# Norms behind the attention by a broadcast ones-product and a wide power on GpSimd, and FFN operands prepared 728 columns at a time

## The chip, the cores and the metric

One core of a Trainium2 chip runs one program. A core has TensorE (PE, matrix products; its weight loads are listed apart as PEld), VectorE (DVE), ScalarE (ACT), GpSimd (POOL) and SyncE (SP), which issues the DMAs here. Each engine executes its own queue in order; engines wait for one another by semaphores. The metric is the device time of the program in microseconds (us), median of three runs; the span is the time from the first to the last instruction in one profiled execution.

## What is computed

One step of a one-layer encoder over 2048 prompt frames and 8 x 16 sample frames, 2176 columns in all, model width 1024, in F32:

```
h   = RMSNorm(x);  p = h @ w_in                       # u, v | q, k, v
A   = u * (tril(W_s) LN(v) + b)                       # gating in chunks of 128
B   = stick-breaking attention, 8 heads x 64          # causal; samples have a cache
mix = concat(RMSNorm(A), RMSNorm(B)) @ w_out;  x += RMSNorm(mix)
up  = RMSNorm(x) @ w_up;  up_c = causal conv, width 3 (per column of up)
x  += RMSNorm((gelu(up_c[:, :2816]) * up_c[:, 2816:]) @ w_down)
# RMSNorm(x) = x * rsqrt(mean(x*x) + 1e-6) * gain
```

## The kernel before

Activations lie transposed: the 128 partitions hold features, the free axis holds frames (columns), so a norm is a sum over partitions and over the feature tiles. A product of full precision is three products of rounded halves (`mm3`: hi x hi, hi x lo, lo x hi), and so every weight tile is split after its load: ScalarE copies the high half (L184), VectorE subtracts it (L185, both inputs in SBUF).

The program has four phases. Phase 1 projects, phase 2 is the attention with the gating filled in between its products; phase 3, the mix stage (from about 1133 us), forms the mix and the residual x1 over six pieces of columns (five of 384, one of 256); phase 4, the FFN (first product at 1347.53 us), goes over three blocks of 726 or 728 columns. A block runs 44 ups (one weight tile each: the product into PSUM `pu`, convolution taps on VectorE L1112) and 40 downs in five groups, whose products are added into the SBUF tile `acc`, of which there is one.

Jobs (one weight tile and its products) run in a list order (`drive`); between jobs, generators in `chains` are each advanced one `yield` by `tick`. A chain's `yield`s therefore set how many jobs lie between its steps in the program; a scheduler then places each engine's instructions.

The norms are such chains. A square is taken on ScalarE and added up over the feature tiles (`sq_step`, L256, mostly on GpSimd) into a tile `acc` of 128 x n. `rstd_chain` then makes the factors in a compact form: per 128 columns one product of the sums with a 128 x 64 block of ones (L209) puts the sums of 128 columns on 128 partitions, one column wide; VectorE makes mean + eps (L212, 128 x m, m at most 4); GpSimd takes the power -0.5 of these m columns (L216); VectorE spreads each over a diagonal (L228, and L231 for the low half); one or two products with ones (L236) bring the factors to all partitions and n columns in PSUM (`rb`), from where VectorE's scalings read them. The chains behind the attention that use it:

- `mix_prep_chain`: norm of a piece of attention output `ob` (scaling L959, residue L963), beside the mix products of the piece before;
- `x1_chain`: norm of the mix (scaling L984, residual add on GpSimd L987);
- `h2_chain`: norm of x1 for the first FFN block (scaling L1010, residues L1016);
- `ffn_prep_chain`: for the next FFN block, first four norms of 182 columns each (`norm_chain`), then, once the last reader of the old operands is done, the operands: for each of four sub-blocks of 182 columns it fetches all 8 feature tiles of x1 and scales, copies and subtracts tile by tile (L920, L923, L924);
- `y_chain` and `y_last_chain`: norm of the FFN output in two parts (scalings L1218 and L1193 in place in `acc`, residual adds, then the stores).

`KEEP` names the tiles of w_out that stay in SBUF through phase 3; the others are fetched and split again for each piece.

Of the kernel before, what the change touches and what calls it, by code (L numbers as in the profile page):

```python
# [34 lines left out]
EPS = 1e-6  # L35
# [18 lines left out]
def hybrid_kernel(ctx: ExitStack, tc: tile.TileContext, a: dict):  # L54
    nc = tc.nc
    dma = nc.sync.dma_start
# [14 lines left out]
    ones = cpool.tile([P, P], F32, name="ones")  # L71
# [127 lines left out]
    def rstd_chain(pool, pspool, key, acc, n, width, shared=None, w=None):  # L199

        starts = [min(s, n - P) for s in range(0, n, P)]
        m = len(starts)
        sh = m * P - n
        yield
        out = pspool.tile([P, 512], F32, tag="st" + key, name="rb", bufs=1)
        for i, s in enumerate(starts):
            nc.tensor.matmul(out[:, 64 * i:64 * i + 64], lhsT=acc[:, s:s + P], rhs=ones[:, 0:64],  # L209
                             start=True, stop=True)  # L210
        var = pool.tile([P, 4], F32, tag="var" + key, name="var", bufs=2)
        nc.vector.tensor_scalar(  # L212
            out=var[:, :m], in0=out[:, :64 * m].rearrange("p (m t) -> p m t", t=64)[:, :, 0],
            scalar1=1.0 / width, scalar2=EPS, op0=ALU.mult, op1=ALU.add)
        r = pool.tile([P, 4], F32, tag="rstd" + key, name="rstd", bufs=2)
        nc.gpsimd.tensor_tensor(out=r[:, :m], in0=var[:, :m], in1=mhalf[:, :m], op=ALU.pow)  # L216
        yield
        yield
        if shared:
            yield from lock(shared)  # L220
        tag = shared or "dg" + key
        parts = 2 if w else 1
        dg = pool.tile([P, 2, w], F32R, tag=tag, name="dg", bufs=1) if w else pool.tile(
            [P, 1, 384], F32, tag=tag, name="dg", bufs=1)
        for i in range(m):
            o = sh if i == m - 1 else 0
            c = slice(i * P, (i + 1) * P - o)
            nc.vector.tensor_scalar(out=dg[:, 0, c], in0=ident[:, o:], scalar1=r[:, i:i + 1],  # L228
                                    scalar2=None, op0=ALU.mult)
            if w:  # L230
                nc.vector.scalar_tensor_tensor(out=dg[:, 1, c], in0=ident[:, o:], scalar=r[:, i:i + 1],  # L231
                                               in1=dg[:, 0, c].bitcast(F32), op0=ALU.mult, op1=ALU.subtract)
        yield
        yield
        for i in range(parts):
            nc.tensor.matmul(out[:, :n], lhsT=onesr if w else ones, rhs=dg[:, i, :n],  # L236
                             start=(i == 0), stop=(i == parts - 1))
        held.discard(shared)
        return r, out

    def norm_chain(pool, pspool, key, src, nk, n, width):
        acc = pool.tile([P, 182], F32, tag="sqa" + key, name="sqa", bufs=1)
        for k0 in range(0, nk, 4):
            sq_sum(pool, key, acc, src[:, k0:k0 + 4, :n], k0 == 0, n)
            yield
        yield
        return (yield from rstd_chain(pool, pspool, key, acc, n, width, w=182))[1]

    def sq_step(pool, key, acc, src, first, n, eng=None):

# [9 lines left out]
    def lock(key):  # L260
# [2 lines left out]
            yield  # L263
        held.add(key)

    def mm3(ps, whi, wlo, ahi, alo, start, stop):
        nc.tensor.matmul(ps, lhsT=whi, rhs=ahi, start=start, stop=False)  # L267
        nc.tensor.matmul(ps, lhsT=whi, rhs=alo, start=False, stop=False)  # L268
        nc.tensor.matmul(ps, lhsT=wlo, rhs=ahi, start=False, stop=stop)  # L269


    kqs = ExitStack()
# [619 lines left out]
    def ffn_prep_chain(pool, pspool, fb, out, free):  # L892

        s0, n0, n1 = FBLK[fb]
        subs = [(o, min(182, n0 + n1 - o)) for o in range(0, n0 + n1, 182)]
        rbs = pool.tile([P, 728], F32, tag="rbs", name="rbs", bufs=1)

        def fetch_x1(off, n):
            x = pool.tile([P, KD, 182], F32, tag="xp", name="xp")
            for src, o0, o1 in x1_s.parts(s0 + off, s0 + off + n):  # L900
                dma(x[:, :, o0:o1], src.rearrange("k p n -> p k n"))
            return x

        for off, n in subs:
            yield from lock("b")
            x = fetch_x1(off, n)
            yield
            rb = yield from norm_chain(pool, pspool, "b", x, KD, n, D)
            nc.vector.tensor_copy(rbs[:, off:off + n], rb[:, :n])
            held.discard("b")  # L910
        nxt = fetch_x1(*subs[0])
        while not free():
            yield
        hhi = hpool.tile([P, KD, 728], F32R, tag="hhi", name="hhi")
        hlo = hpool.tile([P, KD, 728], F32R, tag="hlo", name="hlo")
        for i, (off, n) in enumerate(subs):
            x, nxt = nxt, fetch_x1(*subs[i + 1]) if i + 1 < len(subs) else None
            for k in range(KD):
                hi, lo = hhi[:, k, off:off + n], hlo[:, k, off:off + n]
                tc.keep_in_program_order(nc.vector.scalar_tensor_tensor(  # L920
                    out=x[:, k, :n], in0=x[:, k, :n], scalar=cvec[:, C_GPF + k:C_GPF + k + 1],
                    in1=rbs[:, off:off + n], op0=ALU.mult, op1=ALU.mult))
                nc.scalar.copy(hi, x[:, k, :n])  # L923
                (nc.gpsimd if k % 2 else nc.vector).tensor_tensor(out=lo, in0=x[:, k, :n], in1=hi.bitcast(F32),  # L924
                                                                  op=ALU.subtract)
                if k % 2:
                    yield
        out += [hhi, hlo]

    ypool = ctx.enter_context(tc.tile_pool(name="y", bufs=1, reuse_waits="tile", side="right"))  # L930
# [1 line left out]
    with ExitStack() as c3:  # L932
# [5 lines left out]
        def mix_prep_chain(pi, A):  # L938
# [15 lines left out]
            for f in range(4):  # L954
                sq_step(two, "x", acc, ob[f], f == 0, n, nc.vector)
            yield
            rb = (yield from rstd_chain(two, ps3s, "a", acc, n, 512, "dg"))[1]
            for f in range(4):
                tc.keep_in_program_order(nc.vector.scalar_tensor_tensor(  # L959
                    out=ob[f], in0=ob[f], scalar=cvec[:, C_GB + f:C_GB + f + 1], in1=rb[:, :n],  # L960
# [6 lines left out]
        def x1_chain(pi, mix, acc):  # L967
# [8 lines left out]
            x = []  # L976
            for k in range(0, 6, 2):
                fetch(k)
            yield
            rb = (yield from rstd_chain(two, ps3s, "x", acc, n, D, "dg"))[1]  # L980
            if pi < 2:
                sumb = two.tile([P, 384], F32, tag="dgb", name="sumb", bufs=1)
            for k in range(KD):
# [16 lines left out]
        def h2_chain(pi, mix, acc):  # L1000
# [2 lines left out]
            n = min(PIECES[pi][1], FBLK[1][0] + 2 - c0)  # L1003
            hhi, hlo = h2
            yield
            rb = (yield from rstd_chain(two, ps3s, "b", acc, n, D))[1]
            parts = [(0, 0, NSAMP), (NSAMP, NSAMP + 2, n - NSAMP)] if pi == 0 else [(0, c0 + 2, n)]
            for k in range(KD):
                t = two.tile([P, 384], F32, tag="h", name="h")
# [60 lines left out]
    with ExitStack() as c4:  # L1070
# [11 lines left out]
        def block_jobs(fb, h2, h2n):  # L1082
# [104 lines left out]
            def y_last_chain(acc, c, pi, ssum):  # L1187
                c0, n = c.start, c.stop - c.start
                x, t0 = st["x"], s0 + 2 + c0
                rb = (yield from rstd_chain(one, psd, "yb"[pi], ssum, n, D, w=(TAIL, 256)[pi]))[1]  # L1190
                for k in range(KD):
                    o, xk = acc[:, k, c], x[:, k, c]
                    tc.keep_in_program_order(nc.vector.scalar_tensor_tensor(  # L1193
# [10 lines left out]
            def y_chain(acc, c, pi, ssum):  # L1204
                c0, n = c.start, c.stop - c.start
                yield from lock("y")
                rb = (yield from rstd_chain(one, psd, "y", ssum, n, D, w=TAIL))[1]
                if first:
                    parts = [(0, 0, NSAMP), (NSAMP + 2, NSAMP, n - NSAMP - 2)] if pi == 0 else [(0, c0 - 2, n)]
                else:  # L1210
# [129 lines left out]
```

## Time and profile before

| | |
|---|---|
| runs | 2986.50, 2989.91, 2989.08 us; median 2989.08 |
| profiled execution | 2982.77 us, span 2981.0 us, mean granted TensorE clock 0.984 |
| busy | PE 2861.2, DVE 1893.1, ACT 1345.9, POOL 336.4 us |
| mix stage, 1133 to 1373 us | PE 233.39, DVE 167.33, ACT 118.26, POOL 118.85 of 240.00 us |
| FFN, 1373 to 2953 us | PE 1567.37, DVE 820.56, ACT 514.28, POOL 82.35 of 1580.00 us |
| last 28 us | PE 11.26, DVE 20.36, ACT 2.51, POOL 12.61 us |

All times of the rows come from the one profiled execution, whose own time is 6.3 us under the median. A row of a group gives busy time and mean duration over all of its instructions; the idle time beside it is what the engine spent waiting just before them, with the releaser. Matmuls overlap in the pipeline, so a matmul's shown duration (about 330 ns for 364 columns) is longer than the distance to the next (about 167 ns).

### The profile page before, as it was taken

To read this page: it belongs to the slowest core of one execution; us is meant where nothing else is said; L and a number is where in the kernel's file an instruction comes from. 1 tells how busy PE (TensorE), PEld (TensorE's weight loads), DVE (VectorE), ACT (ScalarE), POOL (GpSimd) and SP (SyncE) were. 2 spreads that over 40 slices of the span, in tenths; PEclk is the share of its full clock that TensorE was granted. 3 is DMA by queue.
4 is the path that set the end of the run, shared out by engine and by line. 5 is a ranking of instruction groups with operands and counts; after the bars stand their busy time and mean duration, and the time that the engine had idled before them with its cause. 6 is when DMAs were issued, how large, how long until landed. Compare 5 with 4: busy or idle time off the path is not lost.

```text
span 2981.0 us, 44269 instructions
## 1 busy us (share of the span) xinstructions
PE 2861.2 (96%) x17094; PEld 2625.7 (88%) x17094; DVE 1893.1 (64%) x2840; ACT 1345.9 (45%) x2391; POOL 336.4 (11%) x487
## 2 busy tenths in 40 slices
PE   9999988889989998999999999999999999999997
PEld 8999876657666768999999999999999989999997
DVE  7666668888988885866454455763444566344445
ACT  5445457677777764554332233433222343323232
POOL 0000011010111012562000000300000030000002
PEclk9999989999999999999999999999999999999998
DMA  7767854322433226665212212532212233221223
GB/s 253 240 231 242 260 168 124 110 86 67 133 87 106 84 70 224 216 208 174 84 58 78 65 61 69 160 118 75 67 57 64 64 115 115 78 64 54 75 64 109
DMA packets 242673, 356.06 MB, mean 119 GB/s; under 512 B 26528, under 2 KB 172192, under 8 KB 241440
## 3 DMA queue, kind: packets, MB, share of 16 engines
q1 hardware_dynamic: 242464, 353.24, 37.9%
q8 instruction: 135, 2.21, 0.3%
q14 instruction: 74, 0.61, 0.1%
HBM read 285.66 MB, written 67.51 MB: 118 GB/s over the span
## 4 chain that ended last, share of the span: by engine, by line
PE 60%; DVE 4%; DMA 2%; ACT 1%; issue 1%; POOL 0%; SPq 0%; POOLq 0%; DVEq 0%; ACTq 0%
PE pu L268 12%; PE pu L267 12%; PE pu L269 12%; PE pd L267 5%; PE pd L269 5%; PE pd L268 5%; PE psm L267 2%; PE psm L268 2%; PE psm L269 2%; PE po L724 1%; PE z L690 1%; PE pt L707 1%; DMA xp<-x_s 1%; DVE S L556 1%; DMA wr<-wdown 1%
## 5 line engine op out<-in xcount | busy, mean ns | idle before, releaser
L185 DVE TENSOR_TENSOR wlo<-wr,whi 128x1024 fp32r<-128x1024 f32 (+2 forms) x325 | 353.6, 1089 | 552.0 <-ACT whi L184 550.1
L267 PE MATMUL pu<-hhi,whi 128*128 128x364 f32 (+1 forms) x2112 | 694.8, 329 | 1.8 <-ACT nhs L1124 1.8
L268 PE MATMUL pu<-hlo,whi 128*128 128x364 f32 (+1 forms) x2112 | 695.4, 329 | 0.0
L269 PE MATMUL pu<-hhi,wlo 128*128 128x364 f32 (+1 forms) x2112 | 694.9, 329 | 0.0
L184 ACT CAST whi<-wr 128x1024 fp32r<-128x1024 f32 (+2 forms) x325 | 297.0, 914 | 699.4 <-PE pu L268 276.0
L267 PEld LDWEIGHTS pu<-hhi,whi 128*128 128x128 f32 x2112 | 398.6, 189 | 2.4 <-ACT nhs L1124 2.4
L268 PEld LDWEIGHTS pu<-hlo,whi 128*128 128x128 f32 x2112 | 398.0, 188 | 0.2 <-POOL hlo L924 0.2
L269 PEld LDWEIGHTS pu<-hhi,wlo 128*128 128x128 f32 x2112 | 397.5, 188 | 0.1
L267 PE MATMUL pd<-ghi,whi 128*128 128x362 f32 (+3 forms) x1016 | 335.8, 330 | 11.9 <-DVE acc L1160 11.8
L269 PE MATMUL pd<-ghi,wlo 128*128 128x362 f32 (+3 forms) x1016 | 334.8, 330 | 0.0
L268 PE MATMUL pd<-glo,whi 128*128 128x362 f32 (+3 forms) x1016 | 334.7, 329 | 0.0
L1112 DVE SCALAR_TENSOR_TENSOR y<-pu,cvec,y 128x726 f32<-128x726 f32 (+2 forms) x352 | 270.0, 777 | 8.7 <-ACT y L1109 4.1
L556 DVE TENSOR_TENSOR_SCAN S<-S 128x896 f32<-128x896 f32 (+8 forms) x136 | 216.6, 1596 | 28.2 <-ACT S L553 27.9
L553 ACT ACTIVATE S<-z 128x512 f32<-128x512 f32 (+3 forms) x336 | 191.2, 572 | 60.4 <-DVE left L698 17.6
L707 PEld LDWEIGHTS pt<-ident,s 128*128 128x128 f32 x1088 | 128.5, 146 | 98.5 <-ACT wT L708 39.9
L707 PE MATMUL pt<-ident,s 128*128 128x128 f32 x1088 | 177.9, 291 | 35.0 <-ACT wT L708 26.1
L690 PE MATMUL z<-K,Q 128*128 128x512 f32 (+3 forms) x640 | 198.6, 409 | 10.0 <-ACT s L554 8.7
L267 PEld LDWEIGHTS pd<-ghi,whi 128*128 128x128 f32 x1016 | 192.5, 189 | 15.4 <-DVE acc L1160 7.3
L558 DVE TENSOR_TENSOR s<-s,S 128x640 f32<-128x640 f32 (+7 forms) x200 | 179.3, 902 | 37.8 <-ACT s L554 23.0
L1160 DVE TENSOR_TENSOR acc<-acc,pd 128x362 f32<-128x362 f32 (+2 forms) x192 | 101.6, 530 | 156.5 <-PE pd L269 155.9
L708 ACT COPY wT<-pt 128x512 f32<-128x512 f32 (+3 forms) x320 | 165.2, 555 | 77.6 <-PE pt L707 75.8
L268 PEld LDWEIGHTS pd<-glo,whi 128*128 128x128 f32 x1016 | 192.3, 189 | 0.3
(212 smaller groups left out, 4938.7 us busy)
## 6 DMA issues: line engine op xcount, KB each, us to landing
wr<-wup SPq DMA_DIRECT2D x132, 512.0 KB, 3.3
wk<-win_t SPq DMA_DIRECT2D x96, 256.0 KB, 2.7
wr<-win_f SPq DMA_DIRECT2D x40, 512.0 KB, 5.0
wr<-wout SPq DMA_DIRECT2D x38, 512.0 KB, 4.1
wr<-wdown SPq DMA_DIRECT2D x72, 256.0 KB, 2.7
x<-xT SPq DMA_DIRECT2D x40, 384.0 KB, 5.1
wr<-wdown SPq DMA_DIRECT2D x48, 320.0 KB, 2.9
Q<-q_s SPq DMA_DIRECT2D x112, 128.0 KB, 4.6
```

The costliest lines, as they stand in the source:

```text
L184: nc.scalar.copy(hi, wr)
L185: nc.vector.tensor_tensor(out=lo, in0=wr, in1=hi.bitcast(F32), op=ALU.subtract)
L267: nc.tensor.matmul(ps, lhsT=whi, rhs=ahi, start=start, stop=False)
L268: nc.tensor.matmul(ps, lhsT=whi, rhs=alo, start=False, stop=False)
L269: nc.tensor.matmul(ps, lhsT=wlo, rhs=ahi, start=False, stop=stop)
L553: nc.scalar.activation(S[:, c0:c0 + cn], z, AF.Sigmoid, scale=-1.0)
L556: nc.vector.tensor_tensor_scan(out=R, data0=R, data1=R, initial=1.0 if carry is None else carry, op0=ALU.mult, op1=ALU.bypass)
L558: nc.vector.tensor_tensor(out=s[:, :W], in0=s[:, :W], in1=S[:, 1:W + 1], op=ALU.mult)
L690: nc.tensor.matmul(z, lhsT=Q[:, j, i * P:(i + 1) * P], rhs=K2[:, b0 * P + c0:b0 * P + c0 + cn], start=(j == 0), stop=(j == 1 and not diago ...
L707: nc.tensor.transpose(pt[:, j], st["w"][:, (j0 - b0 + j) * P:(j0 - b0 + j + 1) * P], ident)
L708: nc.scalar.copy(shared["T", pr, j0, g][:, :jn, i * P:(i + 1) * P], pt[:, :jn])
L1112: nc.vector.scalar_tensor_tensor(out=o, in0=i, scalar=w, in1=o, op0=ALU.mult, op1=ALU.add)
```

## The change

Behind the attention the compact form is replaced by `bcast_chain`. One F32 product of a full 128 x 128 block of ones with the sums over all n columns gives the sum of every column on every partition; VectorE makes mean + eps over n columns from PSUM into an SBUF tile `rw`; GpSimd takes the power of these 128 x n in place; the scalings read `rw` from SBUF. No diagonals are made and no second product. The norms of phase 1 keep `rstd_chain`. The widths are 384 (256 in the last piece, 340 for the second part of the first FFN block's operands), 182, 362 and 364, and 470 and 256 in the last block.

The products of the 182-column norms are issued behind the newest block product (`newest`). In `ffn_prep_chain` the second part now fetches two feature tiles over all 728 columns (`fetch_pair`) and scales, copies and subtracts each over 728 columns: 8 steps of 728 columns in place of 32 of 182, the same elements. Its very first fetch goes through `load`, which keeps the order of the weight loads. `KEEP` loses one tile. Both `rw` and a 128 x 470 tile of -0.5 are new in SBUF.

```diff
+    mhalfw = cpool.tile([P, 470], F32, name="mhalfw")
+    nc.gpsimd.memset(mhalfw, -0.5)
+
+    def bcast_chain(pool, pspool, key, acc, n, width, w):
+
+        yield
+        out = pspool.tile([P, 512], F32, tag="st" + key, name="rb", bufs=1)
+        with tc.issue_after(newest[0]) if w == 182 else ExitStack():
+            nc.tensor.matmul(out[:, :n], lhsT=ones, rhs=acc[:, :n], start=True, stop=True)
+        r = pool.tile([P, w], F32, tag="rw" + key, name="rw", bufs=1)
+        nc.vector.tensor_scalar(out=r[:, :n], in0=out[:, :n], scalar1=1.0 / width, scalar2=EPS, op0=ALU.mult,
+                                op1=ALU.add)
+        nc.gpsimd.tensor_tensor(out=r[:, :n], in0=r[:, :n], in1=mhalfw[:, :n], op=ALU.pow)
+        yield
+        yield
+        return r
...
-        return (yield from rstd_chain(pool, pspool, key, acc, n, width, w=182))[1]
+        return (yield from bcast_chain(pool, pspool, key, acc, n, width, 182))
...
+        newest[:] = [nc.tensor.matmul(ps, lhsT=wlo, rhs=ahi, start=False, stop=stop).ins]
...
-            x = fetch_x1(off, n)
+            x = fetch_x1(off, n, dma if off else load)
...
+        def fetch_pair(k):
+            x = pool.tile([P, KD * 182], F32, tag="xp", name="xw").rearrange("p (k n) -> p k n", k=2)
+            for src, o0, o1 in x1_s.parts(s0, s0 + total):
+                dma(x[:, :, o0:o1], src[k:k + 2].rearrange("k p n -> p k n"))
+            return x
...
-        for i, (off, n) in enumerate(subs):
-            x, nxt = nxt, fetch_x1(*subs[i + 1]) if i + 1 < len(subs) else None
-            for k in range(KD):
-                hi, lo = hhi[:, k, off:off + n], hlo[:, k, off:off + n]
+        for k0 in range(0, KD, 2):
+            x, nxt = nxt, fetch_pair(k0 + 2) if k0 + 2 < KD else None
+            for j in range(2):
+                k, xk = k0 + j, x[:, j, :total]
+                hi, lo = hhi[:, k, :total], hlo[:, k, :total]
...
-            rb = (yield from rstd_chain(two, ps3s, "a", acc, n, 512, "dg"))[1]
+            rb = yield from bcast_chain(two, ps3s, "a", acc, n, 512, 384)
...
-            rb = (yield from rstd_chain(two, ps3s, "x", acc, n, D, "dg"))[1]
+            rb = yield from bcast_chain(two, ps3s, "x", acc, n, D, 384)
...
-            rb = (yield from rstd_chain(two, ps3s, "b", acc, n, D))[1]
+            rb = yield from bcast_chain(two, ps3s, "b", acc, n, D, 384)
...
-        KEEP = (0, 2)
+        KEEP = (0,)
...
-                rb = (yield from rstd_chain(one, psd, "yb"[pi], ssum, n, D, w=(TAIL, 256)[pi]))[1]
+                rb = yield from bcast_chain(one, psd, "yb"[pi], ssum, n, D, (TAIL, 256)[pi])
...
-                rb = (yield from rstd_chain(one, psd, "y", ssum, n, D, w=TAIL))[1]
+                rb = yield from bcast_chain(one, psd, "y", ssum, n, D, TAIL)
```

In the new kernel the line numbers are others: the wide mean + eps is L252 and the wide power L254, the square sums L274, the residual add of the mix L1014, its scaling L1011, the taps L1139, the scalings of the y chains L1245 and L1220, the last residual adds L1224. Three places of the instruction order follow.

GpSimd in the mix stage, in the kernel before, from the norm of the second piece of `ob` on (`rstd` is the narrow power's result, `sumx` the mix's sum of squares, `mix<-x,mix` the residual adds):

```order
L216 TENSOR_TENSOR rstd<-var,mhalf 128x3
L256 TENSOR_TENSOR sumx<-sumx,sq_12132 128x384
L216 TENSOR_TENSOR rstd<-var,mhalf 128x3
L256 TENSOR_TENSOR sumx<-sumx,sq_12179 128x384
L987 TENSOR_TENSOR mix<-x,mix 128x384 x8
L256 TENSOR_TENSOR sumx<-sumx,sq_12237 128x384
L256 TENSOR_TENSOR sumx<-sumx,sq_12301 128x384
L256 TENSOR_TENSOR sumx<-sumx,sq_12347 128x384
L256 TENSOR_TENSOR sumx<-sumx,sq_12384 128x384
L216 TENSOR_TENSOR rstd<-var,mhalf 128x3
```

The same stretch of GpSimd in the changed kernel (`rw` is the tile of n factors):

```order
L254 TENSOR_TENSOR rw<-rw,mhalfw 128x384
L274 TENSOR_TENSOR sumx<-sumx,sq_12121 128x384
L254 TENSOR_TENSOR rw<-rw,mhalfw 128x384
L1014 TENSOR_TENSOR mix<-x,mix 128x384 x8
L274 TENSOR_TENSOR sumx<-sumx,sq_12179 128x384
L274 TENSOR_TENSOR sumx<-sumx,sq_12242 128x384
L274 TENSOR_TENSOR sumx<-sumx,sq_12288 128x384
L274 TENSOR_TENSOR sumx<-sumx,sq_12328 128x384
L254 TENSOR_TENSOR rw<-rw,mhalfw 128x384
```

Three powers stood here in ten rows, each of 3 columns; now three stand here, each of 384, and the residual adds and the sums of the next piece are still queued in between and behind them.

VectorE in the first y chain, in the kernel before, from the variance on (`var`, `dg`: variance and diagonals; `y<-pu`: taps of an up; `acc<-acc,cvec,rb`: the first scaling of the FFN output):

```order
L212 TENSOR_SCALAR var<-rb 128x3
L192 TENSOR_TENSOR sq<-sq 128x364
L194 TENSOR_TENSOR sqa<-sq 128x182
L228 TENSOR_SCALAR dg<-ident,rstd 128x128 x2
L228 TENSOR_SCALAR dg<-ident,rstd 128x106
L231 SCALAR_TENSOR_TENSOR dg<-ident,rstd,dg 128x128 x2
L231 SCALAR_TENSOR_TENSOR dg<-ident,rstd,dg 128x106
L185 TENSOR_TENSOR wlo<-wr,whi 128x1024
L1112 SCALAR_TENSOR_TENSOR y<-pu,cvec,y 128x726
L192 TENSOR_TENSOR sq<-sq 128x364
L1112 SCALAR_TENSOR_TENSOR y<-pu,cvec,y 128x726
...
L1218 SCALAR_TENSOR_TENSOR acc<-acc,cvec,rb 128x362
```

The same in the changed kernel, where `rw<-rb` is the mean + eps over 362 columns and 18 rows, the taps of six more ups and what belongs to them, are left out:

```order
L252 TENSOR_SCALAR rw<-rb 128x362
L185 TENSOR_TENSOR wlo<-wr,whi 128x1024
L1139 SCALAR_TENSOR_TENSOR y<-pu,cvec,y 128x726 x2
L185 TENSOR_TENSOR wlo<-wr,whi 128x1024
...
L1139 SCALAR_TENSOR_TENSOR y<-pu,cvec,y 128x726 x2
L1158 TENSOR_TENSOR y<-y 128x726
L172 TENSOR_TENSOR glo<-y,ghi 128x726
L1245 SCALAR_TENSOR_TENSOR acc<-acc,cvec,rw 128x362 x4
L1249 TENSOR_TENSOR xr<-xr,acc 128x128
```

The first scaling stood behind the taps of one up; it now stands behind those of eight ups, and all four scalings of the first half together.

GpSimd at the end of the program, in the kernel before (`sumy`: sums of squares of the FFN output, `xl`: the last residual adds):

```order
L256 TENSOR_TENSOR sumy<-sumy,sq_27516 128x256
L256 TENSOR_TENSOR sumy<-sumy,sq_27533 128x256
L216 TENSOR_TENSOR rstd<-var,mhalf 128x4
L256 TENSOR_TENSOR sumy<-sumy,sq_27559 128x256
L256 TENSOR_TENSOR sumy<-sumy,sq_27576 128x256
L256 TENSOR_TENSOR sumy<-sumy,sq_27597 128x256
L256 TENSOR_TENSOR sumy<-sumy,sq_27616 128x256
L1197 TENSOR_TENSOR xl<-xl,acc 128x470 x2
L216 TENSOR_TENSOR rstd<-var,mhalf 128x2
L1197 TENSOR_TENSOR xl<-xl,acc 128x470 x2
L1197 TENSOR_TENSOR xl<-xl,acc 128x256 x4
```

And in the changed kernel:

```order
L274 TENSOR_TENSOR sumy<-sumy,sq_27178 128x256
L274 TENSOR_TENSOR sumy<-sumy,sq_27195 128x256
L254 TENSOR_TENSOR rw<-rw,mhalfw 128x470
L274 TENSOR_TENSOR sumy<-sumy,sq_27214 128x256
L274 TENSOR_TENSOR sumy<-sumy,sq_27233 128x256
L1224 TENSOR_TENSOR xl<-xl,acc 128x470
L274 TENSOR_TENSOR sumy<-sumy,sq_27252 128x256
L1224 TENSOR_TENSOR xl<-xl,acc 128x470
L274 TENSOR_TENSOR sumy<-sumy,sq_27272 128x256
L1224 TENSOR_TENSOR xl<-xl,acc 128x470
L254 TENSOR_TENSOR rw<-rw,mhalfw 128x256
L1224 TENSOR_TENSOR xl<-xl,acc 128x470
```

The power of the first part (470 columns) stood before four sums of the second part and still does; the adds of the first part and the sums of the second are now mixed behind it, and the second power stands behind them.

## Rows read from the trace of the kernel before

**Rows 1.** The page, part 1: busy us (share of the span), instructions, by engine.
```profile
PE 2861.2 (96%) x17094; PEld 2625.7 (88%) x17094; DVE 1893.1 (64%) x2840; ACT 1345.9 (45%) x2391; POOL 336.4 (11%) x487
```

**Rows 2.** Windows by stage: length, busy time (instructions) by engine, clock, DMA.
```profile
1133.00:1373.00 240.00, 233.39 (x1399) 227.46 (x1398) 167.33 (x265) 118.26 (x225) 118.85 (x110) 0.99 0.65 217
1373.00:2953.00 1580.00, 1567.37 (x9384) 1561.46 (x9383) 820.56 (x1262) 514.28 (x766) 82.35 (x94) 1.00 0.26 81
2953.00:2981.00 28.00, 11.26 (x80) 9.94 (x78) 20.36 (x45) 2.51 (x6) 12.61 (x16) 0.72 0.29 106
```

**Rows 3.** Timeline of GpSimd: start, duration, what; the narrow powers, four places.
```profile
1120.44 0.55 POOL L791 TENSOR_TENSOR rs<-ms,mhalf 128x1 f32<-128x1 f32 x1 [6.38 <-DVE ms L789]
...
1295.62 0.86 POOL L216 TENSOR_TENSOR rstd<-var,mhalf 128x3 f32<-128x3 f32 x1 [3.93 <-DVE var L212]
1297.88 0.70 POOL L216 TENSOR_TENSOR rstd<-var,mhalf 128x2 f32<-128x2 f32 x1 [1.41 <-DVE var L212]
...
2955.24 1.01 POOL L216 TENSOR_TENSOR rstd<-var,mhalf 128x4 f32<-128x4 f32 x1
```

**Rows 4.** Groups of GpSimd instructions by shape: count, busy us, mean ns, idle.
```profile
L987 POOL TENSOR_TENSOR mix<-x,mix 128x384 f32<-128x384 f32 x40 | 46.7, 1198 | 1.5 <-DVE mix L984 1.5
L256 POOL TENSOR_TENSOR sumx<-sumx,sq 128x384 f32<-128x384 f32 x30 | 39.2, 1308 | 56.8 <-ACT sq L255 56.5
...
L216 POOL TENSOR_TENSOR rstd<-var,mhalf 128x3 f32<-128x3 f32 x21 | 18.9, 899 | 191.8 <-DVE var L212 191.8
...
L216 POOL TENSOR_TENSOR rstd<-var,mhalf 128x2 f32<-128x2 f32 x12 | 9.4, 785 | 138.8 <-DVE var L212 138.8
```

**Rows 5.** Timelines of GpSimd and TensorE: first mix power, first up products.
```profile
1134.97 0.86 POOL L216 TENSOR_TENSOR rstd<-var,mhalf 128x3 f32<-128x3 f32 x1 [11.72 <-DVE var L212]
...
1347.53 0.34 PE L267 MATMUL pu<-hhi,whi 128*128 128x362 f32 x1
1347.70 0.32 PE L268 MATMUL pu<-hlo,whi 128*128 128x362 f32 x1
```

**Rows 6.** Windows: two block turns of the FFN, and the mix stage's beginning.
```profile
1847.00:1877.00 30.00, 24.35 (x141) 23.22 (x141) 22.32 (x48) 14.37 (x36) 12.25 (x18) 1.00 0.36 112
2379.00:2426.00 47.00, 41.05 (x240) 39.61 (x240) 34.77 (x74) 22.66 (x52) 18.77 (x22) 1.00 0.37 110
1124.00:1133.00 9.00, 0.83 (x3) 0.87 (x4) 4.12 (x5) 2.97 (x6) 0.00 (x0) 0.50 1.02 319
1133.00:1147.00 14.00, 14.00 (x74) 13.56 (x73) 6.43 (x13) 3.54 (x5) 0.86 (x1) 0.89 0.75 263
```

**Rows 7.** Timelines of GpSimd and VectorE; last, VectorE's group of weight splits.
```profile
1238.81 1.33 POOL L256 TENSOR_TENSOR sumx<-sumx,sq 128x384 f32<-128x384 f32 x1
...
1239.18 2.04 DVE L185 TENSOR_TENSOR wlo<-wr,whi 128x1024 fp32r<-128x1024 f32 x1
...
1264.16 0.85 POOL L216 TENSOR_TENSOR rstd<-var,mhalf 128x3 f32<-128x3 f32 x1 [0.71 <-DVE var L212]
...
1264.48 1.21 DVE L185 TENSOR_TENSOR wlo<-wr,whi 128x1024 fp32r<-128x1024 f32 x1
...
L185 DVE TENSOR_TENSOR wlo<-wr,whi 128x1024 fp32r<-128x1024 f32 x210 | 264.9, 1262 | 353.4 <-ACT whi L184 353.0
```

**Rows 8.** Timelines of TensorE and ScalarE around the first y chain.
```profile
1897.02 0.44 PE L209 MATMUL rb<-ones,sumy 128*128 128x64 f32 x3
...
1991.76 0.46 ACT L1158 COPY acc<-pd 128x362 f32<-128x362 f32 x1 [1.11 <-PE pd L269]
```

**Rows 9.** Groups by shape: TensorE's norm products, VectorE's scaling behind them.
```profile
L209 PE MATMUL rb<-ones,sumx 128*128 128x64 f32 x34 | 4.4, 265 | 0.0
...
L236 PE MATMUL rb<-dg,ones 128*128 128x384 f32 x22 | 9.1, 494 | 2.0 <-DVE dg L228 2.0
...
L984 DVE SCALAR_TENSOR_TENSOR mix<-mix,cvec,rb 128x384 f32<-128x384 f32 x40 | 21.7, 606 | 7.6 <-PE rb L236 7.6
```

More of the change, by code (lines that the diff above doesn't have):

```diff
@@ L207, in rstd_chain @@
         out = pspool.tile([P, 512], F32, tag="st" + key, name="rb", bufs=1)
-        for i, s in enumerate(starts):
-            nc.tensor.matmul(out[:, 64 * i:64 * i + 64], lhsT=acc[:, s:s + P], rhs=ones[:, 0:64],
-                             start=True, stop=True)
+        with tc.issue_after(newest[0]) if key == "b" and w else ExitStack():
+            for i, s in enumerate(starts):
+                nc.tensor.matmul(out[:, 64 * i:64 * i + 64], lhsT=acc[:, s:s + P], rhs=ones[:, 0:64],
+                                 start=True, stop=True)
         var = pool.tile([P, 4], F32, tag="var" + key, name="var", bufs=2)
@@ L264, in lock @@
         held.add(key)
+    newest = []
     def mm3(ps, whi, wlo, ahi, alo, start, stop):
@@ L896, in ffn_prep_chain, with fetch_x1 @@
         rbs = pool.tile([P, 728], F32, tag="rbs", name="rbs", bufs=1)
-        def fetch_x1(off, n):
-            x = pool.tile([P, KD, 182], F32, tag="xp", name="xp")
+        def fetch_x1(off, n, get=dma):
+            x = pool.tile([P, KD * 182], F32, tag="xp", name="xp").rearrange("p (k n) -> p k n", k=KD)
             for src, o0, o1 in x1_s.parts(s0 + off, s0 + off + n):
-                dma(x[:, :, o0:o1], src.rearrange("k p n -> p k n"))
+                get(x[:, :, o0:o1], src.rearrange("k p n -> p k n"))
             return x
@@ L910, in ffn_prep_chain @@
             held.discard("b")
-        nxt = fetch_x1(*subs[0])
+        total = n0 + n1
+        def fetch_pair(k):
[3 more added lines that the diff above has]
+            return x
+        nxt = fetch_pair(0)
         while not free():
@@ L915, in ffn_prep_chain @@
         hlo = hpool.tile([P, KD, 728], F32R, tag="hlo", name="hlo")
-        for i, (off, n) in enumerate(subs):
-            x, nxt = nxt, fetch_x1(*subs[i + 1]) if i + 1 < len(subs) else None
-            for k in range(KD):
-                hi, lo = hhi[:, k, off:off + n], hlo[:, k, off:off + n]
-                tc.keep_in_program_order(nc.vector.scalar_tensor_tensor(
[L921 to L927, printed above, removed]
+        for k0 in range(0, KD, 2):
[3 more added lines that the diff above has]
+                hi, lo = hhi[:, k, :total], hlo[:, k, :total]
+                tc.keep_in_program_order(nc.vector.scalar_tensor_tensor(
+                    out=xk, in0=xk, scalar=cvec[:, C_GPF + k:C_GPF + k + 1],
+                    in1=rbs[:, :total], op0=ALU.mult, op1=ALU.mult))
+                nc.scalar.copy(hi, xk)
+                (nc.gpsimd if j else nc.vector).tensor_tensor(out=lo, in0=xk, in1=hi.bitcast(F32), op=ALU.subtract)
+                yield
         out += [hhi, hlo]
```

1 line of the change is left out of this document (removed).

## The prediction

> **What bounds the kernel now.** I read the busy shares first, then the windows by stage, and then, for each place the change touches, the timeline of the engine concerned. TensorE is busy for 96% of the span and GpSimd for 11% [rows 1]. By stage [rows 2]: in the mix stage (1133 to 1373 us) TensorE works 233.39 of 240.00 us and GpSimd 118.85; in the FFN TensorE works 1567.37 of 1580.00 and GpSimd 82.35; only the last 28 us belong to others. So TensorE bounds everything up to 2953, and a norm costs time only if its result comes after TensorE, or a chain that holds up its buffers, has run out of other work. The share that tempts one is GpSimd's 11%: it seems to have room for anything. But the room lies in the FFN; in the mix stage some 121 us are free.
>
> **The wide power.** Behind attention the root of a norm is now taken by one GpSimd power over all n columns, where it was a power of 2 to 4 columns. There are 28: in the mix stage 14 (eleven of 384 columns, one of 340, two of 256), eight of 182 for FFN operands, four of 362 or 364 and one each of 470 and 256 behind FFN blocks. No row shows a wide power. The narrow ones, where nothing else held them, took 0.55 us for 1 column, 0.70 for 2, 0.86 for 3 and 1.01 for 4 [rows 3]: each further column cost (1.01 - 0.55)/3 = 0.153 us, with no sign of flattening. From below, a GpSimd add over 384 columns takes 1308 or 1198 ns [rows 4]: all columns of an add cost about what five of a power do. From above, 0.55 + 0.153 x 383 = 59.15 us for 384. The ends are a factor 45 apart. I take the upper one, since the power is the same operation on the same engine; the add shows what moving the data costs, the powers what the root costs. (By the group means, 899 ns at 3 columns and 785 at 2 [rows 4], a column is 0.114 us, and 384 make 44.2.) So 340 columns take 52.4, 256 take 39.6, 182 take 28.2, 362 and 364 take 55.8 and 56.1, 470 take 72.3.
>
> **Mix stage.** The 14 powers take 11 x 59.15 + 52.4 + 2 x 39.6 = 782.3 us. GpSimd runs its queue in order, and the sums of squares and the residual adds stand between the powers, so nothing overtakes. The next norm needs what the last one scaled: ob norm, mix product, sum, x1 norm, h2 norm. Read down the changed order, the 13 gaps between powers hold scalings, products and adds of 1 to 22 us, at their durations of before, 157 us in all. The first power began at 1134.97 and the first up product at 1347.53 [rows 5]; an up is 48 products at about 0.17 us, 8.05 us with its ends, so the fourth up began at about 1373. VectorE's scaling behind the last mix power stands before the second up's taps, so it is the fourth up that finds no buffer until that power is done: 1135 + 782 + 157 = 2074. Delay: 2074 - 1373 = 701; with some 5 us for restarts at the low clock, 706. The restart is bounded by the stage's beginning: after the wait there TensorE had 0.50 of its clock, and 0.89 in the next 14 us [rows 6].
>
> **What the wide power keeps VectorE from.** An add on GpSimd does more than occupy GpSimd: beside the add that began at 1238.81 and took 1.33 us, the weight split begun at 1239.18 took 2.04, against 1.26 on average, and ended 1.08 us after the add [rows 7]. The split has two SBUF inputs and did not get on until the add was through. But beside the narrow power at 1264.16 a split took 1.21 [rows 7], as alone. Two readings: the narrow power is past its reading when the split comes (it reads 3 columns), and a wide one, which reads 384 in turn, holds the split for most of its 59 us; or a power never holds it. I take the first, because what the split waits for in an add is a stream of operands, and the wide power has one as long as the add's. The Trainium skill ("SBUF — State Buffer", section "SBUF: two separate sides") says that a GpSimd operation and a VectorE operation with two SBUF inputs exclude each other for the whole instruction, whichever starts first. The add's row agrees with it and the narrow power's does not; no run here shows a wide one. By it the time is the forecast's, without it the first rival's.
>
> If the split is held: in the mix stage about half of VectorE's 167.33 us [rows 2] (splits, residues) no longer lies beside the powers but between them, +80. In the FFN, each 182-column power stops the weights: what stands ready lasts about one job, 8 us, and 2 us of the one in hand, so 28.2 - 10 = 18.2, eight times, 146. The four powers of the y chains leave 56 - 10 = 46 each, 184.
>
> **The y chains** if the split is not held: the sum's product ran at 1897.02, and the next group's first copy into acc, whose one buffer the chain still reads, at 1991.76, 94.7 us later [rows 8]. In VectorE's new order the scalings of the first part stand behind the taps of eight ups (8 x 8.05 and the product, about 66 us), so its own 0.8 + 55.8 is hidden. The second sum then has its turn at about 81 us, 138 with its 56.1, and 148 when it is scaled: 53 late, 106 over two blocks. Held, the 184 above stand in place of these 106.
>
> **Tail.** The 4-column power began at 2955.24 [rows 3]; with 0.5 for the wider variance the one of 470 begins at 2955.7 and ends at 3028.0. Sums and adds queued behind it on GpSimd end at 3034.6, the power of 256 at 3074.2; with about 10 us of scalings, adds and stores behind it that is 3083.9 in place of 2981.0: +103. Nothing hides it, since hardly a product is left; VectorE's residual adds, if held, make it +108.
>
> **What goes.** Per mix norm three sum products (265 ns each, half of it overlapped) and one over the diagonals (494 ns) [rows 9] become one of full width: at most 6 us over the program. VectorE loses diagonals that lay beside TensorE's work: nothing. The scalings read their factor from SBUF instead of PSUM (606 ns at 384 columns [rows 9]): between -0.1 and +0.1 us each, beside waits: nothing. FFN operands in 8 wide steps per block instead of 32: at the two block turns TensorE idled 5.65 and 5.95 us [rows 6], so between 0 and -12; I take -6. One more weight tile fetched per piece (KEEP): 1.26 us of splitting [rows 7] beside a piece's products (233.39 / 6 = 39 us); nothing without a hold, inside the +80 with it. The fetches of FFN operands stay on SP's queue, in as many bytes; the product of an operand norm, now placed behind a block product, follows it on TensorE's own queue and adds no wait on another.
>
> **Sum.** Against the profiled execution, 2982.8 us: 706 + 80 + 146 + 184 + 4 (restarts) + 108 - 12 (6 of products, 6 at the turns) = 1216, so 4199. The median of the three runs shown, 2989.1, lies 6.3 higher: **4205 us**.
>
> **Rivals.**
> *The power holds nothing.* 2982.8 + 706 + 106 + 4 + 103 - 12 = 3890, median 3896; the 182-column powers are hidden then, since about 32 us of ups or 35 us of downs stand ahead of each consumer. With 0.114 us a column it is about 3640. For it: the split beside the narrow power. Against: the split beside the add.
> *The power is as cheap as the add.* If the cost per column is the start of a vector loop that flattens at width, 384 columns take 1.2 to 1.3 us [rows 4], less than what goes: the mix norm's power, diagonals and second product together are longer. Then nothing waits and the gains are left: -12 at the turns (5.65 + 5.95) and -17 of products, 2954, median 2960: faster. It decides from about 3 us per wide power downward. For it: the adds' rate. Against: four widths on a straight line. The Trainium skill ("GPSIMD Engine Reference", section 3.1) gives an add 4497 ns for 2048 elements, by which 384 would be 0.84 us, an estimate; the adds here took 1.2 to 1.3, and no page prices a power.
> *Steps of several columns overlap*, 0.04 us each: 384 make about 15, 14 of them 200; about 120 of these fit in the stage's free GpSimd time, the tail costs some 27: 3090.
>
> **How the numbers follow.** The held power 0.55 (4050 to 4450, 4205 the middle), the one that holds nothing 0.30 (3600 to 3950), the overlap 0.05, the cheap one 0.05, longer than 4500 (the power stretched when a split comes first) 0.05. The range 3600 to 4480 leaves out under 2 in 10. Only the cheap case is faster. A change under 0.2%, 6 us, can't be told from none; it would need a power of about 3 us: 0.01. Faster 0.05, same 0.01, slower 0.94.
>
> **What would show it.** GpSimd busy near 1600 us in place of 336; the power over 384 columns near 59 us; the mix stage some 900 us long with TensorE under a third busy, and its waits ending on VectorE's scalings and on the power; splits of 28 us and more beside powers if they are held, 1.2 if not. The forecast is wrong if the 384-column power takes under 20 us, and wrong in its second half if TensorE stands still for less than 50 us at the operand norms of the FFN.

## The result and the profile after

The changed kernel takes **3943.69 us** (median of 4 runs, 3938.55 to 3946.80) against 2987.79 before (the three runs shown ahead and a fourth): ratio 1.3204, 95% interval 1.3189 to 1.3220, so 956 us slower. The profiled execution has a span of 3943.1 us and a mean TensorE clock of 0.864.

The page's busy line, and of its chain of waits the shares by engine and the beginning of those by line (answers to [rows 1]):

```profile
PE 2894.2 (73%) x16946; PEld 2642.2 (67%) x16946; DVE 1903.0 (48%) x2665; ACT 1347.2 (34%) x2348; POOL 1713.2 (43%) x464
...
PE 39%; POOL 22%; issue 8%; DVE 4%; DMA 2%; ACT 1%; SPq 0%; POOLq 0%; DVEq 0%; ACTq 0%
POOL rw L254 20%; PE pu L288 8%; PE pu L287 8%; PE pu L289 8%; PE pd L287 4%; PE pd L289 4%; PE pd L288 4%; POOL mix L1014 1%; PE po L744 1%; DMA xw<-x_s 1%; DVE S L576 1%; PE pt L727 1%; POOL sumx L274 1%; PE z L710 1%; DMA wr<-wdown 0%
```

GpSimd's busy time has grown from 336.4 to 1713.2 us, and line 254, the wide power, is alone on the path for a fifth of the span. TensorE does the same work as before (2894 us against 2861) in a longer time.

The windows of the three stages, with their new ends (columns as in [rows 2]: length, busy time of PE, PEld, DVE, ACT, POOL, granted clock, DMA share, GB/s):

```profile
1137.00:2116.00 979.00, 267.54 (x1331) 247.27 (x1330) 190.30 (x230) 126.81 (x230) 919.26 (x110) 0.62 0.17 55
2116.00:3784.00 1668.00, 1548.12 (x9219) 1542.32 (x9219) 796.08 (x1121) 499.05 (x704) 531.76 (x64) 0.97 0.25 76
3784.00:3944.00 160.00, 27.41 (x164) 24.08 (x163) 30.56 (x47) 9.19 (x18) 137.84 (x22) 0.59 0.07 24
```

The mix stage was 240 us with TensorE at 233; here it is 979 with TensorE at 268 and GpSimd at 919. Its clock share is 0.62, so the products that remain also ran partly at the low level.

The groups of the wide power by width (count, busy us, mean ns, idle before), which answer to [rows 3, 4]:

```profile
L254 POOL TENSOR_TENSOR rw<-rw,mhalfw 128x384 f32<-128x384 f32 x11 | 681.9, 61992 | 42.5 <-DVE rw L252 42.5
L254 POOL TENSOR_TENSOR rw<-rw,mhalfw 128x182 f32<-128x182 f32 x8 | 235.6, 29446 | 566.1 <-DVE rw L252 566.1
L254 POOL TENSOR_TENSOR rw<-rw,mhalfw 128x256 f32<-128x256 f32 x3 | 124.4, 41471 | 2.3 <-DVE rw L252 2.3
...
L254 POOL TENSOR_TENSOR rw<-rw,mhalfw 128x470 f32<-128x470 f32 x1 | 75.5, 75486 | 0.0
```

From 256 to 470 columns a column costs (75.49 - 41.47)/214 = 0.159 us, from 182 to 384 (61.99 - 29.45)/202 = 0.161: the line that four narrow powers drew, at 0.153, holds over a hundredfold in width.

First and last power of the mix stage and the first product of the fourth up, from the timelines of GpSimd and TensorE (answer to [rows 5]):

```profile
1139.74 61.71 POOL L254 TENSOR_TENSOR rw<-rw,mhalfw 128x384 f32<-128x384 f32 x1 [15.53 <-DVE rw L252]
...
2060.06 41.23 POOL L254 TENSOR_TENSOR rw<-rw,mhalfw 128x256 f32<-128x256 f32 x1 [2.35 <-DVE rw L252]
...
2113.70 0.67 PE L287 MATMUL pu<-hhi,whi 128*128 128x362 f32 x1 [34.20 <-ACT nhs L1151]
```

The waits of TensorE in the mix stage (what it waited for: us in all, times, longest):

```profile
PE psm L287 <- ACT ahi L989: 350.0, 7, 103.7
PE rb L250 <- DVE sumx L274: 142.5, 5, 48.9
PE psm L287 <- ACT mix L1064: 136.3, 2, 68.2
```

Each of these is one hop from the power: the ob norm that ScalarE rounds (`ahi`), the sum whose chain stands behind GpSimd's queue, the PSUM that is free when ScalarE has copied the mix. The same view from 2116 us to the end:

```profile
PE pd L287 <- ACT acc L1185: 110.0, 2, 55.7
PE rb L250 <- DVE sumy L274: 78.1, 1, 78.1
```

Two waits of 55.7 and 54.3 us for `acc` behind the y chains, one of 78.1 in the tail. No row here names a weight split; in the mix stage's whole list such waits come to 2.1 us.

**Where the 962 us of span went**, from one product to the same one in the other kernel: first mix product, 1132.2 to 1136.1 us, +3.9; from there to the fourth up, 241.6 to 977.6, +736.0; to the first up of the second block, 510.2 to 504.0, -6.2; second block 537.8 to 601.3, +63.5; third block to its last product 540.4 to 591.5, +51.1; from there to the end 18.8 to 132.5, +113.7.

### The profile page after: what moved, and what is told of

It reads as the page before. It is cut to its first block, busy times and chain, and to the rows that moved or that the text cites. A ratio compares the mean times of both kernels' runs of the same rounds, so it can differ in the third digit from the quotient of the medians.

```text
span 3943.1 us, 43704 instructions
## 1 busy us (share of the span) xinstructions
PE 2894.2 (73%) x16946; PEld 2642.2 (67%) x16946; DVE 1903.0 (48%) x2665; ACT 1347.2 (34%) x2348; POOL 1713.2 (43%) x464
## 4 chain that ended last, share of the span: by engine, by line
PE 39%; POOL 22%; issue 8%; DVE 4%; DMA 2%; ACT 1%; SPq 0%; POOLq 0%; DVEq 0%; ACTq 0%
POOL rw L254 20%; PE pu L288 8%; PE pu L287 8%; PE pu L289 8%; PE pd L287 4%; PE pd L289 4%; PE pd L288 4%; POOL mix L1014 1%; PE po L744 1%; DMA xw<-x_s 1%; DVE S L576 1%; PE pt L727 1%; POOL sumx L274 1%; PE z L710 1%; DMA wr<-wdown 0%
## 5 line engine op out<-in xcount | busy, mean ns | idle before, releaser
L254 POOL TENSOR_TENSOR rw<-rw,mhalfw 128x384 f32<-128x384 f32 (+6 forms) x28 | 1406.2, 50223 | 625.4 <-DVE rw L252 625.4
L287 PE MATMUL psm<-ahi,whi 128*128 128x384 f32 (+1 forms) x384 | 136.3, 368 | 500.4 <-ACT ahi L989 350.0
L287 PEld LDWEIGHTS psm<-ahi,whi 128*128 128x128 f32 x384 | 80.6, 213 | 508.7 <-ACT ahi L989 353.3
L1139 DVE SCALAR_TENSOR_TENSOR y<-pu,cvec,y 128x726 f32<-128x726 f32 (+2 forms) x352 | 270.0, 777 | 18.6 <-ACT y L1136 14.0
L274 POOL TENSOR_TENSOR sumy<-sumy,sq 128x362 f32<-128x362 f32 (+3 forms) x36 | 42.3, 1180 | 424.3 <-ACT sq L273 423.8
L566 POOL MEMSET S<- 128x1 f32 x136 | 13.5, 100 | 444.7 <-DVE s L578 317.5
```

The costliest lines, as they stand in the source:

```text
L254: nc.gpsimd.tensor_tensor(out=r[:, :n], in0=r[:, :n], in1=mhalfw[:, :n], op=ALU.pow)
L274: (eng or nc.gpsimd).tensor_tensor(out=acc[:, :n], in0=acc[:, :n], in1=sq[:, :n], op=ALU.add)
L1139: nc.vector.scalar_tensor_tensor(out=o, in0=i, scalar=w, in1=o, op0=ALU.mult, op1=ALU.add)
```

## The experiments

Each ratio below is against the kernel before, run again beside the experiment (medians of 2986.55 to 2987.57 us). The theory that the experiments test: the loss is the length of the powers, in series in the mix stage, behind two blocks and at the end; they do not keep VectorE from its second input, but for a moment. The rivals: the power holds VectorE (the forecast), or other parts of the change cost as well.

**Multiplications in place of the powers** (`e1_mult`).

```diff
-        nc.gpsimd.tensor_tensor(out=r[:, :n], in0=r[:, :n], in1=mhalfw[:, :n], op=ALU.pow)
+        nc.gpsimd.tensor_tensor(out=r[:, :n], in0=r[:, :n], in1=mhalfw[:, :n], op=ALU.mult)
```

> All 28 wide powers become multiplications by -0.5 of the same operands (leaves the root out of these norms; nothing else is changed). Theory A (the whole loss is the length of the powers, 1406 us of GpSimd that stand in series in the mix stage, behind two FFN blocks and at the end; the powers keep VectorE from its port only while they read their operands, about 1.1 us at 384 columns): 2955 to 2985 us, the wide multiplication takes 1.0 to 1.4 us at 384 columns, and a weight split begun beside one is late by up to the rest of it. Theory B (the rest of the change costs too: scalings that read two SBUF tiles, 841 ns in the changed kernel against 606, the fifth reload of a w_out tile per piece): over 3000 us.

Measured 2997.55 us, ratio 1.0037 (1.0026 to 1.0048). So 946 of the 956 us are the powers. But 11 us remain over the kernel before that ran beside it (2986.55), between the two theories and against my forecast for the rest of the change, -12. This pair of runs also bears on the hold. In the changed kernel, the first power of 182 columns and the splits beside it (timelines of GpSimd and VectorE):

```profile
2417.11 29.48 POOL L254 TENSOR_TENSOR rw<-rw,mhalfw 128x182 f32<-128x182 f32 x1 [308.46 <-DVE rw L252]
...
2417.21 1.07 DVE L185 TENSOR_TENSOR wlo<-wr,whi 128x512 fp32r<-128x512 f32 x1
...
2421.50 0.69 DVE L185 TENSOR_TENSOR wlo<-wr,whi 128x512 fp32r<-128x512 f32 x1
...
2438.17 1.23 DVE L185 TENSOR_TENSOR wlo<-wr,whi 128x1024 fp32r<-128x1024 f32 x1
```

In this run, the multiplication at the same place one block later, and the split beside it:

```profile
2229.80 0.62 POOL L254 TENSOR_TENSOR rw<-rw,mhalfw 128x182 f32<-128x182 f32 x1 [264.02 <-DVE rw L252]
...
2229.89 1.08 DVE L185 TENSOR_TENSOR wlo<-wr,whi 128x512 fp32r<-128x512 f32 x1
```

The split of 512 columns begun 0.10 us after the power took 1.07 us, where the next one took 0.69; the one begun 0.09 us after the multiplication, which lasted 0.62, took 1.08. So the power costs a split begun beside its start as much as a multiplication of its width does, 0.38 us. For the other 29 us nothing is held: splits took 0.69 and, over 1024 columns, 1.23. It is so all over the changed kernel: 68 splits of 1024 columns begun more than 2.5 us into a power took 1.22 to 1.23 us, 15 of 512 took 0.68 to 0.70.

What is lost at the start grows with the power's width. A VectorE subtraction with two SBUF inputs (L1043, 340 columns) beside a power of 384 columns, and the next one of its kind (timelines of GpSimd and VectorE in the changed kernel):

```profile
1710.67 61.94 POOL L254 TENSOR_TENSOR rw<-rw,mhalfw 128x384 f32<-128x384 f32 x1 [1.86 <-DVE rw L252]
...
1710.98 1.30 DVE L1043 TENSOR_TENSOR hlo<-h,hhi 128x340 fp32r<-128x340 f32 x1
...
1713.43 0.51 DVE L1043 TENSOR_TENSOR hlo<-h,hhi 128x340 fp32r<-128x340 f32 x1 [0.54 <-ACT hhi L1042]
```

The same place in the run with half of the columns (`e10_half`, below), where the power has 192:

```profile
1466.62 31.25 POOL L254 TENSOR_TENSOR rw<-rw,mhalfw 128x192 f32<-128x192 f32 x1 [1.86 <-DVE rw L252]
...
1466.93 0.89 DVE L1043 TENSOR_TENSOR hlo<-h,hhi 128x340 fp32r<-128x340 f32 x1
```

The loss is 0.79 us beside 384 columns, 0.38 beside 192 and 0.38 beside 182, some 0.002 us a column. That a power reads all its operands first and then works on them is what I infer; no row shows the reading.

**Only the FFN operands wide** (`e5_wideops`: `ffn_prep_chain` as in the changed kernel, all else as before).

> The kernel before with only the FFN operands prepared over 728 columns (fetch of two feature tiles, 8 wide steps for 32), all norms compact. Theory A (the turns of the blocks lose idle time of TensorE, 5.65 and 5.95 us before, 3.8 us seen at the second turn of the changed kernel): 2979 to 2987 against 2988. Theory B (turn hidden or wide steps late for the first ups): 2988 to 2995.

Measured 2981.30 us, ratio 0.9980 (0.9972 to 0.9989): theory A. Fetching and preparing two feature tiles over 728 columns is worth some 5 us (2986.55 beside it). Of TensorE's idle time at the two turns 3.2 us went: 3.16 and 5.27 us are left of 5.65 and 5.95. The other part shows in the clock: at the first turn of the profiled execution before, it fell to its low level for 3.4 us, here it did not.

**Compact norms in the mix stage** (`e2_mixnarrow`).

```diff
-            rb = yield from bcast_chain(two, ps3s, "a", acc, n, 512, 384)
+            rb = (yield from rstd_chain(two, ps3s, "a", acc, n, 512, "dg"))[1]
...
-            rb = yield from bcast_chain(two, ps3s, "x", acc, n, D, 384)
+            rb = (yield from rstd_chain(two, ps3s, "x", acc, n, D, "dg"))[1]
...
-            rb = yield from bcast_chain(two, ps3s, "b", acc, n, D, 384)
+            rb = (yield from rstd_chain(two, ps3s, "b", acc, n, D))[1]
```

> The changed kernel with the compact norms in the mix stage alone (ob, mix and x1 norms, 14 powers of 2 or 3 columns); FFN operands, y chains and the end keep the wide power. Theory A (14 powers in series are the stage's delay, 740 us by the fourth up): 3944 - 740 = 3204, between 3190 and 3220. Theory B (part of the stage's delay is the other edits there, a reload more per piece and scalings from SBUF): over 3230.

Measured 3210.53 us, ratio 1.0743 (1.0727 to 1.0760): 733 us come back, as theory A had it. TensorE's longest waits from 1370 us on stay those of the FFN:

```profile
PE pd L287 <- ACT acc L1185: 113.3, 2, 57.1
PE rb L250 <- DVE sumy L274: 78.1, 1, 78.1
```

**Compact norms behind the FFN** (`e4_ynarrow`: the same edit in `y_chain` and `y_last_chain`).

> The changed kernel with the compact norms behind the FFN alone (four y chains, two at the end); mix stage and operand norms keep the wide power. Theory A (stalls of 55.7 and 54.3 us with some 4 us of restart each, and 114 us at the end): 3944 - 232 = 3712, between 3700 and 3722. Theory B (the stalls come from the operand norms before them or from the order of the blocks): the end alone returns, about 3830.

Measured 3716.37 us, ratio 1.2439 (1.2421 to 1.2457): 227 us come back, the two waits for `acc` and the tail, again theory A. Together with the run before, 733 + 227 = 960 of 956: the parts add up. What is left at the head of TensorE's waits from 1370 us on is the mix stage alone:

```profile
PE psm L287 <- ACT ahi L989: 254.9, 5, 103.7
PE rb L250 <- DVE sumx L274: 142.5, 5, 48.9
PE psm L287 <- ACT mix L1064: 136.3, 2, 68.2
```

**Compact norms for the FFN operands** (`e3_opnarrow`: the same edit in `norm_chain`).

> The changed kernel with compact norms for the FFN operands alone (eight powers of 182 columns become powers of 2). Theory A (a power holds VectorE only in its first 0.6 us, and its 29 us are hidden behind ups and downs): 3936 to 3950, no change against 3944. Theory H, the forecast's (a power holds the splits all along): 3944 - 146 = 3798.

Measured 3946.61 us, ratio 1.3212 (1.3192 to 1.3232): no change. Eight powers of 29 us cost nothing, and the forecast's 146 us are refuted.

**Half of the columns** (`e10_half`).

```diff
-        nc.gpsimd.tensor_tensor(out=r[:, :n], in0=r[:, :n], in1=mhalfw[:, :n], op=ALU.pow)
+        nc.gpsimd.tensor_tensor(out=r[:, :n // 2], in0=r[:, :n // 2], in1=mhalfw[:, :n // 2], op=ALU.pow)
```

> The changed kernel with every wide power over half of its columns (leaves the root out of the other half). Theory A (0.16 us a column, in series): mix stage 2538 columns fewer, -405; the two stalls of the y chains 29 shorter each, -58; the end 363 columns fewer, -58; 3944 - 521 = 3423, between 3405 and 3440. Rival (a fixed part per power, such as the start of a loop, is most of it): above 3600.

Measured 3368.38 us, ratio 1.1279 (1.1264 to 1.1295), 55 below what theory A gave. The groups of the power by width:

```profile
L254 POOL TENSOR_TENSOR rw<-rw,mhalfw 128x192 f32<-128x192 f32 x11 | 344.5, 31315 | 42.0 <-DVE rw L252 42.0
L254 POOL TENSOR_TENSOR rw<-rw,mhalfw 128x91 f32<-128x91 f32 x8 | 119.1, 14883 | 558.7 <-DVE rw L252 558.7
```

0.160 us a column again, with well under 1 us of fixed part, and from the first mix product to the fourth up 574.4 us against 977.6: -403, as expected. The end, 74.5 us against 132.5, also came as expected. The miss is in the y chains, where no wait for `acc` over 2 us is left instead of two of some 26. The program's order had moved: VectorE's mean + eps of both parts and the first scalings between them (timeline of VectorE)

```profile
2227.75 0.53 DVE L252 TENSOR_SCALAR rw<-rb 128x362 f32<-128x362 f32 x1 [1.16 <-PE rb L250]
...
2259.97 2.11 DVE L1245 SCALAR_TENSOR_TENSOR acc<-acc,cvec,rw 128x362 f32<-128x362 f32 x4
...
2274.76 0.53 DVE L252 TENSOR_SCALAR rw<-rb 128x364 f32<-128x364 f32 x1
```

The scalings stand 32 us behind the variance here; in the changed kernel, behind eight ups, it was some 65. I had held the order fixed while I changed an instruction by which the scheduler sets it.

**What the other 11 us are.** In the run with multiplications the mix stage, first product to fourth up, took 259.6 us against 241.6 before. Its scalings of 384 columns, and TensorE's largest wait in the stage:

```profile
L1011 DVE SCALAR_TENSOR_TENSOR mix<-mix,cvec,rw 128x384 f32<-128x384 f32 x40 | 45.0, 1190 | 2.2 <-POOL rw L254 2.2
```

```profile
PE psm L289 <- DVE wlo L185: 14.1, 5, 4.8
```

A scaling took 606 ns in the kernel before [rows 9]. Two edits were undone in that run, each alone and then both; the first keeps two w_out tiles (`e11_keep`), the second brings the factors back to PSUM in the mix stage (`e12_psum`).

```diff
-        KEEP = (0,)
+        KEEP = (0, 2)
```

```diff
+        if w == 384:
+            nc.scalar.copy(out[:, :n], r[:, :n])
...
-        return r
+        return out if w == 384 else r
```

> As the run with multiplications (it leaves the root out, 2997.6 us), with KEEP back at two resident w_out tiles. That run lost 19 us in the mix stage, with TensorE waiting 14.1 us for weight splits there. Theory K (the extra reload and split per piece cost them): 2980 to 2986. Theory S (the scalings, whose factor now lies in SBUF, wait for GpSimd's adds, 841 ns against 606): 2993 to 2998, since the splits saved are 5 x 1.26 us of VectorE alone. Theory O (the new order of the steps): 2997.

> As the run with multiplications (it leaves the root out, 2997.6 us), but in the mix stage ScalarE copies the factors back into the PSUM tile of the product, and the scalings read them there, as in the kernel before. Theory S: scalings near 606 ns again, 2982 to 2988. Theory K or O: 2997 or, with the copy's half microsecond in 14 chains, up to 3003.

> The run with factors copied back into PSUM (it leaves the root out, 2976.1 us) with two resident w_out tiles. If the reload costs by itself what it cost there (2997.6 - 2985.6 = 12): 2964. If it cost only because VectorE was late from the held scalings: 2973 to 2978, no change.

Measured 2985.62 us (0.9991, 0.9980 to 1.0001) with two tiles kept, 2976.05 (0.9963, 0.9951 to 0.9976) with PSUM factors, 2968.64 (0.9937, 0.9924 to 0.9950) with both. The stage took 253.2, 239.6 and 232.8 us in the profiles: the factors in SBUF cost 20 us (259.6 - 239.6; 253.2 - 232.8), the reload 6 to 7 (259.6 - 253.2; 239.6 - 232.8), and in the profiles the two add up, so neither K nor S alone was right and the reload does not need late scalings to cost. By the medians the factors are worth 21.5 and 17 us and the reload 12 and 7; the reload is the less certain of the two. The forecasts held in part: with two tiles the time is in K's range, with PSUM factors it is 6 us under that of S, and with both it lies between the two values given. Their sum hid what the wide form without its root saves there, 241.6 - 232.8 = 9 us. The scalings with PSUM factors:

```profile
L1013 DVE SCALAR_TENSOR_TENSOR mix<-mix,cvec,rb 128x384 f32<-128x384 f32 x40 | 21.6, 606 | 3.3 <-ACT rb L256 3.3
```

The same shape, the same count, half the time. With its factor in SBUF a scaling has two SBUF inputs, and it is long where it meets the residual add that GpSimd runs on the tile before: in the run with multiplications 37 of the 40 met work of GpSimd and took 1.24 us in the mean, the three that met none 0.62. With the factor in PSUM 37 met it too and took 0.61.

**Another root** (`e14_sqrt`).

```diff
+        nc.scalar.activation(r[:, :n], out[:, :n], AF.Sqrt, scale=1.0 / width, bias=epsv[:, 0:1])
+        nc.vector.reciprocal(out[:, :n], r[:, :n])
...
-        return r
+        return out
```

> The wide form with another root: ScalarE takes the square root of mean + eps from the product's PSUM tile, VectorE the reciprocal back into that tile, the scalings read PSUM as before; two resident w_out tiles; FFN operands over 728 columns. Theory A (with the power gone and the factors in PSUM the wide form costs the mix stage nothing): 2966 to 2980, under the kernel before. Rival (the activation tables that the square root loads, 1.28 us where one was seen, and a second chain step on ScalarE hold up evictions in the mix stage): 2985 to 3010.

Measured 2978.49 us, ratio 0.9964 (0.9952 to 0.9977): under both kernels, in theory A's range. Some 5 of these 9 us are the FFN operands, by the run with them alone; its interval (0.9972 to 0.9989) overlaps this one, so a gain of the wide norms themselves is not shown. The tables it loads and the root itself (groups of ScalarE), and the reciprocal (group of VectorE):

```profile
L252 ACT ACT_TABLE_LOAD x10 | 12.8, 1283 | 3.8 <-PE rb L250 3.6
...
L252 ACT ACTIVATE rw<-rb,epsv 128x384 f32<-128x384 f32 x11 | 6.4, 578 | 9.6 <-PE rb L250 9.6
...
L253 DVE RECIPROCAL rb<-rw 128x384 f32<-128x384 f32 x11 | 28.1, 2557 | 14.2 <-ACT rw L252 14.2
```

A square root of 384 columns is 0.58 us here and its reciprocal 2.56, together 3.1 where GpSimd's power is 61.99. It stays 10 us above the run with PSUM factors, two kept tiles and no root (2968.64). In the profiles the mix stage took 240.1 us against 232.8 there and 241.6 in the kernel before, so nearly all that the wide form saved is gone again. The table loads are not the reason in this stage: of the ten, one lies there (at 1135.73 us). VectorE was busy for 178.87 of 240 us of it against 161.49 of 233; its reciprocals may be the reason, but no run parts them from the rest, and the cause of the 10 us stays open.

## Why the prediction was wrong and right

- **Direction and range** held, the 4205 us did not: the case that came is the first rival, *the power holds nothing*, at 3896 with a chance of 0.30. It is 48 us off. The range held because it was drawn over both cases; 0.55 of the chance lay on the one that did not come.
- **The price of the wide power** was right: 59.15 us at 384 columns, measured 61.99. Taking the narrow power's slope over the add's rate, a factor 45 apart, was the decision that mattered, and the same operation on the same engine was the nearer row.
- **Mix stage**: forecast +706, measured +736. The powers were longer (11 x 61.99 + 54.69 + 2 x 41.4 = 819 us against 782), the gaps shorter (142 against 157), and 12 us lay between the last power and the fourth up, where 5 were put for restarts. The gaps' sum was read down the row order.
- **The step that failed** is *what the wide power keeps VectorE from*. From the add that held a split I concluded that a power holds it "for most of its 59 us", because it reads 384 columns "in turn". The stage's 80, the operand norms' 146 and the y chains' other 78 did not come: TensorE waited 2.1 us for splits in the stage, compact operand norms changed nothing (3946.61 us), and the y chains cost what they cost without a hold. The narrow power's row [rows 7] was the better witness, and it allowed a third reading that I did not weigh: all operands are read at the start, however wide. By the Trainium skill's rule ("SBUF — State Buffer", section "SBUF: two separate sides") the hold lasts for the whole instruction; for the add of [rows 7] and the multiplication of 182 columns that agrees with the rows to within 0.2 us, for a power of 29.48 us, beside which splits took 0.69 and 1.23, it does not.
- **The y chains** without a hold: 53 late per block, measured 55.7 and 54.3, and by the steps that were forecast: in the first chain the second power began 80 us behind the first sum's product (forecast 81), and the copy into `acc` 151 behind it (148). **Tail**: +103, measured +113.7; powers of 75.49 and 41.63 us for 72.3 and 39.6 make 5 of it.
- **What goes**, forecast -12, came to +11 without the powers. The -6 at the turns came as -5 (2981.30), of which the idle time there is 3.2. The saving put at 6 for the products was 9 in the mix stage, seen only with the root left out. The scalings that read SBUF were put at "nothing", from -0.1 to +0.1 us each: in the run with multiplications they are 0.6 us longer when GpSimd's adds run beside them, 20 us in the stage. The prediction had the cause in hand, the held split of [rows 7], and did not apply it to the scalings that the change itself turned into operations with two SBUF inputs. The reloaded tile, "nothing without a hold", was 6 to 7 in the profiles.

## What to carry to other kernels

An engine's share of the span says nothing of a new instruction's price: take it from the nearest rows of the same operation, extrapolate by width, and ask whether a chain puts it in series. Whoever moves an operand from PSUM to SBUF should look at what GpSimd runs beside its readers. Before a wide function goes to an engine, price its whole form there: here a square root and a reciprocal took 3.1 us over 384 columns on two engines, the power 62 on one.

## What the runs showed of the hardware

- GpSimd's power: 0.16 us per column of 128 partitions from 91 to 470 columns, against 1.21 us in the mean for a whole multiplication of 384 (0.003 us a column).
- It holds back a VectorE operation with two SBUF inputs only at its start: one begun 0.1 to 0.4 us into it lost 0.38 us at 182 columns and 0.79 at 384, one begun more than 2.5 us into it nothing. A multiplication of 182 columns cost a split the same 0.38 us, though it lasts 0.6 us and not 29.
- A VectorE scaling over 384 columns with two SBUF inputs took 1.24 us in the mean beside GpSimd's adds and 0.62 without; with one input in PSUM it took 0.61 either way.
- ScalarE's square root over 384 columns from PSUM took 0.58 us, a table load 1.28, and VectorE's reciprocal over 384 columns 2.56.
